# Evacuation of keys: both casts of ScalarE first, then both low parts of VectorE

## The chip, the cores and the metric

The kernel runs on one core of one Trainium2 chip. The metric is device time in microseconds (us) of one execution; times of the kernel before and after are medians of several runs. Engines are named as in the profile: PE is TensorE (matrix products), ACT is ScalarE, DVE is VectorE, POOL is GpSimd, SP is SyncE, which issues most DMAs.

## The reference, cut to what matters

One layer over 1024 tokens with width 1024. The input is normalised and modulated, then one projection gives queries, keys, values and gates for 16 heads of width 64: eight heads of forgetting attention (a softmax with a decay added to the scores) and eight of stick-breaking attention (a running product of sigmoids over the keys). The head outputs are gated, projected once more, added to the input and normalised again.

```python
h = u @ w_in[layer]
fq, fk, fv, fg, ff, sq, sk, sv, sg = _split_columns(h)
s = jnp.einsum('bhqd,bhkd->bhqk', q, k).astype(jnp.float32) * scale      # both kinds of heads
s = s + (f_q[..., :, None] - f_k[..., None, :])                          # forgetting heads
log_keep = jnp.where(strict, jax.nn.log_sigmoid(-z), 0.0)                # stick-breaking heads
y = jnp.concatenate([y_fox, y_sb], axis=-1) @ w_out[layer]
```

Everything is float32.

## The kernel before, in words

**Two parts for each number.** PE works here on a rounded 32-bit type (`F32R`). To keep more digits, the kernel splits an operand into a high part, which is the number rounded to that type, and a low part, the difference between the number and its high part. A product then takes several matmuls: high by high, low by high, high by low. The high part is usually a cast on ACT (or POOL), the low part a subtraction on DVE (or POOL).

**Pairs and chunks.** Heads are handled in eight pairs (`p`); a pair's two heads of 64 rows fill the 128 partitions. Pairs 0 to 3 are stick-breaking, 4 to 7 forgetting. For each pair the queries, keys and gates (`m` = 0, 1, 2) are projected in two chunks (`ch`) of 512 tokens. One chunk is 24 matmuls into one accumulator in PSUM (lines 255 to 257 in `m_step`); accumulators are a ring of two buffers (`acc_tile`). When the last matmul of a chunk is done, `evac_m` takes the result out of PSUM.

**Evacuation of keys.** `evac_k` handles a chunk of keys, once for each head in `heads`. Line 240 casts the head's 64 rows of the accumulator to the tile of high keys (`kst`, ACT). Line 242 copies these rows to the other 64 partitions of the same tile (a DMA on SP's queue). Line 243 subtracts the high part from the accumulator and writes the low keys (`klo`, DVE). It returns the last cast and the last subtraction, so that a caller can queue work behind them. Most calls handle both heads: one chunk of pair 0 in the first stage, the second chunks of pairs 0 and 1 after it, and both chunks of pairs 2 to 7 in the generator `gen_m`. Two calls, for the first chunk of pair 1, handle one head each, between other steps.

**Order of the work.** PE's instructions stay in the order in which the program writes them (`manual_schedule`); in the first stage SP's do too. For ACT, DVE, POOL and later SP, a planner chooses the order of instructions by a simulated clock, and adds the waits. In the main part, the attention of a pair runs unit by unit (a unit is one head and 128 queries), and the projections of later pairs fill PE's time in between (`fill`). For unit k the steps are: scores (`att_scores`, lines 410 and 411, one buffer for scores), their processing on ACT, DVE and POOL (lines 417 to 445), and two units later the transposes (line 461), split into a high part (line 463, ACT) and a low part (line 464, DVE), and the products with the values (line 476). In `att_pv` the products with the high part come first. Value projections (lines 310 to 312) use the same ring of accumulators.

Of the kernel before, what the change touches and what calls it, by code (L numbers as in the profile page):

```python
# [8 lines left out]
F32 = mybir.dt.float32  # L9
F32R = mybir.dt.float32r  # L10
AF = mybir.ActivationFunctionType
ALU = mybir.AluOpType
# [6 lines left out]
HD = 64  # L19
# [8 lines left out]
def tile_hybrid_layer(  # L28
# [17 lines left out]
    nc = tc.nc  # L46
# [188 lines left out]
    def evac_k(p, ch, acc, kst, klo, heads):  # L235
        s = slice(ch * 512, ch * 512 + 512)
        for h in heads:
            r = slice(h * HD, h * HD + HD)
            o = slice((1 - h) * HD, (1 - h) * HD + HD)
            first = nc.scalar.copy(kst[h][r, s], acc[r, :])  # L240
            kf = kst[h].bitcast(F32)
            nc.sync.dma_start(kf[o, s], kf[r, s])
            last = nc.vector.tensor_tensor(klo[r, s], acc[r, :], kf[r, s], op=ALU.subtract)  # L243
        return first, last

    def evac_g(p, ch, acc, sg):
# [12 lines left out]
    qst, kst, klo, sgt, vt = {}, {}, {}, {}, {}  # L259
# [11 lines left out]
    def evac_m(p, m, ch, acc, heads=(0, 1)):  # L271
        if m == 0:
            evac_q(p, ch, acc, qst[p], heads)
        elif m == 1:
            return evac_k(p, ch, acc, kst[p], klo[p], heads)
        else:
            evac_g(p, ch, acc, sgt[p])
# [364 lines left out]
    for kb in range(NB):  # L642
        last = kb == NB - 1
# [100 lines left out]
    for kb in range(NB):  # L744
# [13 lines left out]
        if kb < len(evacs):  # L758
            n, h = evacs[kb]
# [209 lines left out]
    for k in range(len(units) + LAG + 1):  # L969
        if k < len(units):  # L970
# [12 lines left out]
            p, h, i = units[k]  # L983
# [86 lines left out]
```

## Time and profile before

| what | us |
|---|---|
| median of 3 runs | 689.89 (689.56 to 691.04) |
| the profiled execution's own time | 689.48 |
| its span in the profile | 687.8 |
| PE busy | 673.6 (98% of the span) |
| DVE, ACT, POOL busy | 451.8, 381.9, 425.8 |
| all 32 casts of line 240 | median 0.58 each |
| all 32 subtractions of line 243 | median 0.69 each |

A row of the timeline gives the start in us from the start of the span, the duration, the engine, the line of the kernel, the operation, output and input, and in brackets the idle time of the engine before it with what released it. On ACT and DVE an instruction's duration overlaps the next one's by about 0.1 us. In the list of waits a row gives the engine and line that waited, what it waited for, the total in us, how often, and the longest. The granted clock of PE was 0.997 over the profiled execution.

### The profile page before, as it was taken

What the parts mean: (1) busy time and instruction counts of PE and PEld (TensorE: products, weight loads), DVE (VectorE), ACT (ScalarE), POOL (GpSimd) and SP (SyncE); (2) the same over time, 40 slices, a digit from 0 to 9 for tenths busy, and PEclk for the clock granted to TensorE, in tenths of its full rate; (3) what the DMA queues carried; (4) which work ended last, traced back from release to release, by engine and by line L of the source; (5) the groups of instructions that cost most, each with busy time, mean ns of one, the idle gap of its engine ahead of it and who ended that gap; (6) DMA issues with size and microseconds to landing.
All of it is one profiled execution on the core that took longest, in us unless ns stands there. A gap on an engine that the chain in (4) does not pass through costs nothing.

```text
span 687.8 us, 11790 instructions
## 1 busy us (share of the span) xinstructions
PE 673.6 (98%) x4033; PEld 589.1 (86%) x4033; DVE 451.8 (66%) x924; ACT 381.9 (56%) x862; POOL 425.8 (62%) x555
## 2 busy tenths in 40 slices
PE   7999999999999999999999999999999999999996
PEld 4789898888998888889998888889988889888885
DVE  6895458767656676767675665656565767774645
ACT  4666457856557666666674564655565666531000
POOL 4567978656438565557388887877584364665411
PEclk9999999999999999999999999999999999999998
DMA  8966231011102122112134553444341298143301
GB/s 306 416 235 246 67 110 57 25 41 53 39 9 70 41 55 55 38 47 62 30 133 150 177 170 109 152 152 147 101 135 54 66 296 350 56 157 117 129 31 61
DMA packets 44316, 81.60 MB, mean 119 GB/s; under 512 B 5152, under 2 KB 18784, under 8 KB 43616
## 3 DMA queue, kind: packets, MB, share of 16 engines
q1 hardware_dynamic: 43104, 76.65, 34.1%
q10 hardware_dynamic: 1152, 4.19, 2.1%
q8 instruction: 32, 0.52, 0.3%
q14 instruction: 28, 0.23, 0.1%
HBM read 60.34 MB, written 16.29 MB: 111 GB/s over the span
## 4 chain that ended last, share of the span: by engine, by line
PE 93%; DVE 2%; DMA 1%; POOL 1%; SPq 1%; ACT 1%; issue 0%; POOLq 0%; DVEq 0%
PE m L255 10%; PE pv L476 10%; PE m L256 10%; PE m L257 10%; PE T L461 9%; PE S L411 5%; PE S L410 5%; PE o L853 4%; PE o L851 4%; PE o L852 4%; PE v L310 4%; PE v L311 4%; PE v L312 4%; DMA wss<-in_w_ss_dram 1%; PE st_q L573 1%; PE st_late L569 1%
## 5 line engine op out<-in xcount | busy, mean ns | idle before, releaser
L255 PE MATMUL m<-uh,whi 128*128 128x512 f32 x304 | 126.5, 416 | 0.5 <-DVE kl L243 0.5
L257 PE MATMUL m<-uh,wlo 128*128 128x512 f32 x304 | 119.7, 394 | 0.0
L256 PE MATMUL m<-ul,whi 128*128 128x512 f32 x304 | 119.7, 394 | 0.0
L464 DVE TENSOR_TENSOR pt<-T,pt 128x512 fp32r<-128x512 f32 (+2 forms) x192 | 100.6, 551 | 17.9 <-ACT pt L463 16.8
L444 POOL TENSOR_TENSOR be<-be,kp 128x127 f32<-128x127 f32 (+3 forms) x64 | 77.1, 1206 | 33.7 <-DVE kp L440 24.0
L463 ACT CAST pt<-T 128x512 fp32r<-128x512 f32 (+2 forms) x192 | 85.7, 480 | 16.8 <-PE T L461 13.0
L436 DVE TENSOR_TENSOR_SCAN kp<-kp,floor 128x512 f32<-128x512 f32 (+2 forms) x64 | 65.2, 1018 | 32.1 <-ACT kp L430 31.2
L476 PEld LDWEIGHTS pv<-pt,v 128*128 128x128 f32 (+1 forms) x640 | 77.1, 163 | 4.5 <-DVE pt L464 0.7
L476 PE MATMUL pv<-pt,v 128*128 128x256 f32 (+3 forms) x640 | 80.4, 271 | 0.5 <-DVE pt L464 0.5
L425 POOL TENSOR_SCALAR a<-a,l 128x1024 f32<-128x1024 f32 (+3 forms) x64 | 48.0, 749 | 39.6 <-DVE l L424 26.0
L257 PEld LDWEIGHTS m<-uh,wlo 128*128 128x128 f32 x304 | 57.1, 188 | 13.6
L423 ACT ACTIVATE a<-a,nm 128x1024 f32<-128x1024 f32 (+3 forms) x64 | 49.8, 778 | 34.1 <-DVE nm L417 33.0
L410 PE MATMUL S<-k,q 128*128 128x512 f32 (+5 forms) x192 | 66.5, 348 | 0.2 <-DVE nm L417 0.2
L411 PE MATMUL S<-kl,qz 128*128 128x512 f32 (+5 forms) x192 | 65.5, 342 | 0.0
L255 PEld LDWEIGHTS m<-uh,whi 128*128 128x128 f32 x304 | 57.3, 188 | 9.2 <-DVE kl L243 0.9
L256 PEld LDWEIGHTS m<-ul,whi 128*128 128x128 f32 x304 | 57.4, 189 | 8.0
L497 POOL TENSOR_TENSOR ty<-ty,sg 64x256 f32<-64x256 f32 x64 | 47.4, 741 | 25.0 <-DVE ty L496 12.8
L417 DVE CUSTOM_DVE_ANT_0 a<-S,fb 128x1024 f32<-128x1024 f32 (+3 forms) x64 | 48.3, 755 | 20.5 <-PE S L411 9.8
L430 ACT ACTIVATE kp<-S 128x128 f32<-128x128 f32 (+3 forms) x64 | 41.7, 651 | 31.8 <-PE S L411 29.7
L310 PE MATMUL v<-whi_v,uh 128*128 128x256 f32 (+1 forms) x192 | 56.1, 292 | 0.7 <-DVE kl L243 0.7
L388 ACT CAST qz<-q 64x128 fp32r<-64x128 f32 x128 | 37.4, 295 | 32.9 <-PE S L411 31.8
L311 PE MATMUL v<-whi_v,ul 128*128 128x256 f32 (+1 forms) x192 | 54.2, 282 | 0.0
(291 smaller groups left out, 1609.6 us busy)
## 6 DMA issues: line engine op xcount, KB each, us to landing
raw<-in_w_qkg_dram SPq DMA_DIRECT2D x38, 256.0 KB, 3.0
wss<-in_w_ss_dram SPq DMA_DIRECT2D x5, 1024.0 KB, 9.0
x<-in_x_dram SPq DMA_DIRECT2D x8, 512.0 KB, 7.6
k<-k SPq DMA_DIRECT2D x32, 128.0 KB, 2.4
wg<-in_w_gate_dram SPq DMA_DIRECT2D x8, 512.0 KB, 4.5
raw_o<-in_w_out_dram SPq DMA_DIRECT2D x16, 256.0 KB, 2.7
fb<-f_dr ACTq DMA_DIRECT2D x8, 512.0 KB, 4.2
wo_dr<-whi_o SPq DMA_DIRECT2D x16, 256.0 KB, 2.7
```

Of the source, the lines that this page charges most:

```text
L255: nc.tensor.matmul(acc, hi[:, c], u_hi[kt][:, s], start=(kt == 0), stop=False)
L256: nc.tensor.matmul(acc, hi[:, c], u_lo[kt][:, s], start=False, stop=False)
L257: nc.tensor.matmul(acc, lo[:, c], u_hi[kt][:, s], start=False, stop=(kt == NB - 1))
L310: nc.tensor.matmul(acc[:, :n], u_hi[kt][:, ts_], hi[:, s], start=(kt == 0), stop=False)
L311: nc.tensor.matmul(acc[:, :n], u_lo[kt][:, ts_], hi[:, s], start=False, stop=False)
L410: nc.tensor.matmul(S[:, s, :w], qst[p][h][:, qs], kst[p][h][:, ks], start=True, stop=False)
L411: nc.tensor.matmul(S[:, s, :w], z, klo[p][:, ks], start=False, stop=True)
L436: scan = nc.vector.tensor_tensor_scan(rv, rv, floor[0][:, 512 - n:][:, ::-1], initial=0.0, op0=ALU.mult, op1=ALU.max)
L444: nc.gpsimd.tensor_tensor(be[:, :ke - 1], be[:, :ke - 1], kp[:, 1:ke], op=ALU.mult)
L463: nc.scalar.copy(hi[:, :n, qo:qo + P], t3)
L464: nc.vector.tensor_tensor(lo[:, :n, qo:qo + P], t3, hi.bitcast(F32)[:, :n, qo:qo + P], op=ALU.subtract)
L476: nc.tensor.matmul(acc[:m, q0:256], vt[p][:, kb, h * P:h * P + m], pt[:, kb % 4, q0:], start=start, stop=stop)
```

## The change

When a call of `evac_k` handles both heads, the program now writes both casts (each with its copy) first and both subtractions after them. Before, it wrote cast, copy, subtraction for head 0 and then the same for head 1. The instructions, their sizes and their tiles are the same. On ACT alone, on DVE alone and on SP's queue alone the instructions of one evacuation keep their sequence; what differs is how those of ACT and DVE stand to each other in the text.

```diff
             first = nc.scalar.copy(kst[h][r, s], acc[r, :])
             kf = kst[h].bitcast(F32)
             nc.sync.dma_start(kf[o, s], kf[r, s])
-            last = nc.vector.tensor_tensor(klo[r, s], acc[r, :], kf[r, s], op=ALU.subtract)
+        for h in heads:
+            r = slice(h * HD, h * HD + HD)
+            last = nc.vector.tensor_tensor(klo[r, s], acc[r, :], kst[h].bitcast(F32)[r, s], op=ALU.subtract)
         return first, last
```

## The prediction, made before the change was run

> **What bounds the kernel now.** I read the page first, then the list of what TensorE (PE) waited for, then who waits for whom around the two lines of the change, then the timelines of PE, ACT and DVE around each evacuation of keys.
>
> ```profile
> span 687.8 us, 11790 instructions
> PE 673.6 (98%) x4033; PEld 589.1 (86%) x4033; DVE 451.8 (66%) x924; ACT 381.9 (56%) x862; POOL 425.8 (62%) x555
> ...
> k<-k SPq DMA_DIRECT2D x32, 128.0 KB, 2.4
> ```
>
> The same order of matmuls with nothing late would take what it takes now less PE's waits. The list of those waits (total, times, longest) is short, and after the first 15 us of loading these are all the groups in it:
>
> ```profile
> PE T L461 <- DVE pt L464: 0.8, 1, 0.8
> PE v L310 <- DVE kl L243: 0.7, 1, 0.7
> PE pv L476 <- DVE pt L464: 0.5, 1, 0.5
> PE m L255 <- DVE kl L243: 0.5, 1, 0.5
> PE S L410 <- DVE nm L417: 0.2, 1, 0.2
> ```
>
> They sum to 2.7 us. Two of the five, 1.2 us, name line 243, the low part of the keys: PE waits there for an accumulator (two buffers) whose last reader is the second low part. So the change can gain about 1.2 us at those two places, 2.7 us if all five went, and no more without other matmuls; what it can lose has no such cap.
>
> How the evacuation runs today is seen where nothing else is on either engine (ACT and DVE timelines: start, duration, operation, idle before and its releaser):
>
> ```profile
> 77.35 0.58 ACT L240 CAST k<-st_late 64x512 fp32r<-64x512 f32 x1 [0.76 <-DVE q L232]
> 78.68 0.58 ACT L240 CAST k<-st_late 64x512 fp32r<-64x512 f32 x1 [0.75 <-DVE kl L243]
> ...
> 77.97 0.68 DVE L243 TENSOR_TENSOR kl<-st_late,k 64x512 fp32r<-64x512 f32 x1 [0.65 <-ACT k L240]
> 79.30 0.69 DVE L243 TENSOR_TENSOR kl<-st_late,k 64x512 fp32r<-64x512 f32 x1 [0.65 <-ACT k L240]
> ```
>
> Cast 0, low part 0, cast 1, low part 1 go strictly one after the other. Cast 1 needs nothing from low part 0, but both read the same accumulator, and cast 1 starts 0.03 us after low part 0 ends (77.97 + 0.68 = 78.65). A handover costs 0.03 to 0.04 us. From first start to last end: 79.99 - 77.35 = 2.64 us.
>
> **The change part by part.** It adds and removes no instruction. Of 17 calls that evacuate keys, 15 do both heads (the 32 copies of the page are 15 x 2 + 2); the two that do one head stay as they are. In the 15, cast 1 no longer stands behind low part 0, and low part 0 now stands behind cast 1, if the readers of one accumulator stay in the order of the text, as they are in the rows above. I take that.
>
> The spacings come from the evacuation at 457.61, whose rows serve again below:
>
> ```profile
> 457.61 0.58 ACT L240 CAST k<-m 64x512 fp32r<-64x512 f32 x1 [1.85 <-PE m L257]
> 458.09 0.47 ACT L463 CAST pt<-T 128x384 fp32r<-128x384 f32 x1
> ...
> 458.22 0.68 DVE L243 TENSOR_TENSOR kl<-m,k 64x512 fp32r<-64x512 f32 x1 [2.27 <-ACT k L240]
> 458.82 0.54 DVE L464 TENSOR_TENSOR pt<-T,pt 128x384 fp32r<-128x384 f32 x1
> 459.29 1.21 DVE L417 CUSTOM_DVE_ANT_0 a<-S,fb 128x1024 f32<-128x1024 f32 x1
> 460.53 0.69 DVE L243 TENSOR_TENSOR kl<-m,k 64x512 fp32r<-64x512 f32 x1
> ...
> 460.08 1.00 PE L476 MATMUL pv<-pt,v 128*128 128x256 f32 x8
> ```
>
> The instruction behind a cast starts 0.48 after it (458.09 - 457.61), the one behind a low part 0.60 after it (458.82 - 458.22). With t the start of cast 0: cast 1 runs from t + 0.48 to t + 1.06, low part 0 starts at t + 1.10 (it was t + 0.62), low part 1 at t + 1.70 and ends at t + 2.39. An undisturbed evacuation is 0.25 us shorter. The copy of head 1 across the partitions issues 0.85 us sooner (from t + 1.91 to t + 1.06), and DMAs behind it on SP's queue by up to that. It lands in 2.4 us. The nearest reader is the first scores, after the copy that issues at 78.68 + 0.58 today:
>
> ```profile
> 91.24 0.22 PE L410 MATMUL S<-k,q 128*128 128x128 f32 x1
> ```
>
> That is 12 us later, so I cost the copies and the queue at nothing; the cover is the projection work between, and would have to shrink to 3 us.
>
> *What goes.* The two accumulator waits:
>
> ```profile
> 171.05 0.58 ACT L240 CAST k<-m 64x512 fp32r<-64x512 f32 x1 [0.74 <-PE m L257]
> 174.11 0.58 ACT L240 CAST k<-m 64x512 fp32r<-64x512 f32 x1
> ...
> 175.67 0.69 DVE L243 TENSOR_TENSOR kl<-m,k 64x512 fp32r<-64x512 f32 x1
> 176.40 1.02 DVE L464 TENSOR_TENSOR pt<-T,pt 128x512 fp32r<-128x512 f32 x2
> ...
> 176.43 0.39 PE L310 MATMUL v<-whi_v,uh 128*128 128x264 f32 x1 [0.74 <-DVE kl L243]
> ...
> 550.14 0.58 ACT L240 CAST k<-m 64x512 fp32r<-64x512 f32 x1 [0.74 <-PE m L257]
> ...
> 552.72 0.69 DVE L243 TENSOR_TENSOR kl<-m,k 64x512 fp32r<-64x512 f32 x1
> 554.22 0.69 DVE L464 TENSOR_TENSOR pt<-T,pt 128x512 fp32r<-128x512 f32 x1
> ...
> 553.47 0.50 PE L255 MATMUL m<-uh,whi 128*128 128x512 f32 x1 [0.47 <-DVE kl L243]
> ```
>
> At 171.05 cast 1 came 3.06 us after cast 0 because other work of ACT had slipped in between; low part 1 ended at 176.36. After the change it ends at 171.05 + 2.39 = 173.44, and PE wants the buffer at 176.43 - 0.74 = 175.69: gone, 0.74 us. At 550.14 it ends at 552.53, PE wants 553.00: gone, 0.47 us. Together -1.21. What is late next at the first place are the differences of line 464; with a low part less ahead of them they end sooner than today's 177.42, so nothing of the 0.74 comes back.
>
> *What is held up.* ACT and DVE now do two things in a row where they had put something else between. ACT's next instruction comes up to 0.48 later, DVE's up to 0.48 + 0.60 later. I followed all 12 evacuations of the main part; at eight the delayed work has over 1 us to spare before PE, at four not.
>
> First, at 261.79, line 431 frees the only scores buffer, with little in hand:
>
> ```profile
> 262.76 0.59 ACT L431 ACTIVATE be<-S 128x512 f32<-128x512 f32 x1
> ...
> 263.68 0.31 PE L410 MATMUL S<-k,q 128*128 128x320 f32 x1
> ```
>
> It ends at 263.35; 0.48 later is 263.83, and with a handover PE starts at 263.87 instead of 263.68: +0.19.
>
> The other three are differences of line 464, the low part of the transposed weights, just ahead of the products (pv) that read them; pv does its high products first (5, 7 and 3 here) at 0.11 us each, then needs the low ones.
>
> ```profile
> 314.05 0.58 ACT L240 CAST k<-m 64x512 fp32r<-64x512 f32 x1 [0.67 <-PE m L257]
> ...
> 315.44 1.00 DVE L464 TENSOR_TENSOR pt<-T,pt 128x512 fp32r<-128x512 f32 x2
> ...
> 316.16 1.47 PE L476 MATMUL pv<-pt,v 128*128 128x256 f32 x12
> ...
> 405.11 0.56 ACT L240 CAST k<-m 64x512 fp32r<-64x512 f32 x1
> ...
> 405.50 0.40 PE L411 MATMUL S<-kl,qz 128*128 128x512 f32 x1
> ...
> 406.31 0.67 DVE L417 CUSTOM_DVE_ANT_0 a<-S,fb 128x512 f32<-128x512 f32 x1
> 406.92 1.14 DVE L464 TENSOR_TENSOR pt<-T,pt 128x512 fp32r<-128x512 f32 x2
> ...
> 407.13 1.97 PE L476 MATMUL pv<-pt,v 128*128 128x256 f32 x16
> ```
>
> At 314.05 the low parts start at 315.15 and 315.75, the first difference at 316.35, ending (0.69) at 317.04. PE needs it at 316.16 + 5 x 0.11 = 316.72, and gets it at 317.08: +0.36. At 405.11 line 417 can go at 405.94 (its scores are done at 405.90), then low parts at 406.55 and 407.15, first difference 407.75 to 408.44; PE needs it at 407.13 + 7 x 0.11 = 407.90: 408.48 makes +0.58. At 457.61 the low parts start at 458.71 and 459.31, and from 459.91 DVE has both line 464 and line 417 waiting. Difference first: it ends at 460.45, PE needs it at 460.08 + 3 x 0.11 = 460.41: +0.08. Line 417 first: 1.14 more (its start to the next start is 460.43 - 459.29 and the idle before it is none), +1.22. I take the first, since the difference is ahead of the scores in the text; both stay in the range.
>
> The Trainium skill (PSUM — Partial Sum Buffer, section Engine vs sequencer instructions) says that the queues of ScalarE and VectorE are strictly first in, first out: by it a low part that waits at the head holds all behind it, which speaks against the change. The trace agrees as far as it goes: ACT stands 0.75 us before the cast at 78.68.
>
> **Sum**: -0.74 - 0.47 + 0.19 + 0.36 + 0.58 + 0.08 = 0.00 us. The profiled execution took 689.48 us around its span of 687.8, the median of the runs is 689.89, 0.41 above it; the forecast is the median unchanged, **689.9 us**. Bounds: without any hold-up -1.21; with line 417 first +1.14.
>
> **The rivals.** (a) *Gain alone*: the planner, which orders ACT and DVE by its own clock, keeps the differences ahead of the low parts, as it does today at 458.82, and the accumulators still come free in time (2.2 and 0.47 us in hand): 689.89 - 1.21 = 688.7. Against: both low parts become ready before the differences at 314 and 457.
>
> (b) *A new wait in place of the old one, slower*: DVE takes the low parts and then also the next scores ahead of the differences: 0.58 + 0.23 at 405 (line 417 behind the low parts, 406.19 + 1.20 + 0.61 = 408.00 instead of 407.75), 1.22 at 457, 0.36 and 0.4 more at 314 (a short scan slips in), 0.19 at 261. That is 2.98 - 1.21 = +1.8: 691.7. It decides from 2.6 us of new PE waits (1.21 + 1.38). For it: cast 1 at 174.11, though first in the text, stands behind work that was ready sooner, so the planner serves by readiness. Against: four places must all fall that way.
>
> (c) *Everything re-planned*: shifted times change the order on ACT, DVE and POOL well beyond the 15 places, and the other three waits (1.5 us) go too: 689.89 - 2.7 = 687.2. Nothing in the trace ties those waits to keys; they end on lines 464 and 417.
>
> (d) *Low part 0 isn't tied to cast 1*: it starts at t + 0.62 as now, 0.48 sooner than assumed. The losses at 314, 405 and 457 shrink to about 0, 0.10 and 0, that at 261 stays: -0.92, 689.0. The Trainium skill (same page, section PSUM bank collisions raise a hardware error) says that readers of different 32-partition quadrants of a bank don't collide, and the heads are 64 partitions apart; the row at 78.68 shows them kept apart all the same, so the trace is stricter.
>
> (e) *It doesn't do what it says*: the planner leaves cast 1 behind other work: 689.9.
>
> **How the numbers follow.** Chances: forecast 0.40, (a) 0.20, (b) 0.20, (c) 0.11, (d) 0.05, (e) 0.04. A measurement of this kernel can tell about 0.2%, 1.4 us, from no change. Forecast, (d), (e) and most of (a) lie within; (c) and a fifth of (a) below; most of (b) above. Faster 0.15, same 0.66, slower 0.19. The range takes in (a) and (b) and leaves out (c) and the far tail of (b): 688.1 to 691.8.
>
> **What would show it.** Right: casts of one evacuation 0.48 apart and low parts 0.60 apart; PE's list without line 243; new short waits for line 464 near 316, 408 and 460 and for line 431 near 263. Wrong: cast 1 still behind lines 430 or 423; waits on line 243 that persist; waits above 0.3 us far from an evacuation (then (c), or its reverse). The prediction is wrong if the time leaves the range, or if it holds because nothing moved rather than because two movements cancel.

## The result, and the profile after

| | before | after |
|---|---|---|
| median, us | 689.61 (5 runs) | 692.18 (5 runs) |
| ratio, 95% interval | | 1.0038 (1.0026 to 1.0049) |
| span of the profiled execution, us | 687.8 | 690.7 |
| PE busy, us | 673.6 | 674.5 |

The change makes the kernel slower by 2.57 us, 0.38%. The forecast was no change, 689.9, and the time lies just outside the range of 688.1 to 691.8. (The forecast started from the first three of the five runs of before, whose median is 689.89.) Lines of the code from the old 244 on are two higher after the change: 245 is the low part of the keys, 397 the causal mask added for a later unit, 412 and 413 the scores, 419 their first step on DVE (the old 417), 433 the second sigmoid, 463 the transposes, 465 and 466 their high and low part, 478 the products with the values. The page counts 16 instructions more than before; all of them are semaphore instructions of the sequencers.

The page of the kernel after, and its list of PE's waits (total, times, longest):

```profile
span 690.7 us, 11806 instructions
PE 674.5 (98%) x4033; PEld 589.3 (85%) x4033; DVE 452.3 (65%) x924; ACT 383.4 (56%) x862; POOL 426.4 (62%) x555
...
PE pv L478 <- DVE pt L466: 3.5, 4, 1.5
...
PE T L463 <- DVE pt L466: 0.8, 1, 0.8
PE S L412 <- ACT be L433: 0.3, 1, 0.3
PE T L463 <- POOL be L447: 0.3, 1, 0.3
PE S L412 <- DVE nm L419: 0.2, 1, 0.2
```

Both waits for the low part of the keys are gone. In their place stand waits of the products for the low part of the transposed weights (0.5 us in one wait before, 3.5 us in four now) and one of the scores for the sigmoid. One of the four is the old wait near 115 us. The other three, and the wait of the scores, are at the four places which the prediction named. Apart from 0.3 us near 97 us, where the transposes wait for POOL right after the first stage (experiment 1 has the changed order there too, and not this wait), there is no new one in the main part. ACT, DVE and PE at these places (rows as before; "x2" is two instructions in a row):

```profile
261.19 1.19 ACT L240 CAST k<-m 64x512 fp32r<-64x512 f32 x2 [0.85 <-PE m L259]
262.40 0.60 ACT L432 ACTIVATE kp<-S 128x512 f32<-128x512 f32 x1
...
263.54 0.41 PE L412 MATMUL S<-k,q 128*128 128x320 f32 x1 [0.30 <-ACT be L433]
...
314.06 1.19 ACT L240 CAST k<-m 64x512 fp32r<-64x512 f32 x2 [0.67 <-PE m L259]
315.27 0.86 ACT L465 CAST pt<-T 128x512 fp32r<-128x512 f32 x2
...
315.28 1.39 DVE L245 TENSOR_TENSOR kl<-m,k 64x512 fp32r<-64x512 f32 x2 [0.33 <-ACT k L240]
316.70 1.02 DVE L466 TENSOR_TENSOR pt<-T,pt 128x512 fp32r<-128x512 f32 x2
...
317.45 0.98 PE L478 MATMUL pv<-pt,v 128*64 128x256 f32 x7 [0.59 <-DVE pt L466]
...
406.79 0.69 DVE L419 CUSTOM_DVE_ANT_0 a<-S,fb 128x512 f32<-128x512 f32 x1 [0.63 <-POOL ty L499]
407.41 1.39 DVE L245 TENSOR_TENSOR kl<-m,k 64x512 fp32r<-64x512 f32 x2
408.82 0.29 DVE L397 TENSOR_TENSOR fb<-fb,ps_causal 128x128 f32<-128x128 f32 x1
409.03 1.15 DVE L466 TENSOR_TENSOR pt<-T,pt 128x512 fp32r<-128x512 f32 x2
...
409.77 1.21 PE L478 MATMUL pv<-pt,v 128*64 128x256 f32 x9 [0.92 <-DVE pt L466]
...
459.50 1.19 ACT L240 CAST k<-m 64x512 fp32r<-64x512 f32 x2 [1.85 <-PE m L259]
460.71 0.48 ACT L465 CAST pt<-T 128x384 fp32r<-128x384 f32 x1
...
460.72 1.39 DVE L245 TENSOR_TENSOR kl<-m,k 64x512 fp32r<-64x512 f32 x2 [2.87 <-ACT k L240]
462.14 1.23 DVE L419 CUSTOM_DVE_ANT_0 a<-S,fb 128x1024 f32<-128x1024 f32 x1
463.29 0.55 DVE L466 TENSOR_TENSOR pt<-T,pt 128x384 fp32r<-128x384 f32 x1
...
460.33 0.40 PE L413 MATMUL S<-kl,qz 128*128 128x512 f32 x1
463.90 0.75 PE L478 MATMUL pv<-pt,v 128*64 128x256 f32 x5 [1.46 <-DVE pt L466]
```

At the first place the two casts run in a row, the sigmoids of lines 432 and 433 start behind them, and PE's scores wait for line 433. The other three show one picture: the two low parts run in a row, the difference of line 466 starts right behind them (or behind line 397 or 419 as well), and PE stops in the middle of a group of products until it is done.

How much each place cost is read from PE's own starts. PE's matmuls stand in the same order in both kernels, so the start of a scores matmul behind each place, after minus before, shows how far PE is late there. It is the first one behind the place, at pair 3 the second (line 413), since the first is the one that waits:

```
scores matmul after ...        before   after    late    step
the first stage                101.15   101.47   +0.32
pair 2, second chunk           181.51   180.91   -0.60   -0.92
pair 3, second chunk           263.82   263.79   -0.03   +0.57
pair 4, second chunk           319.65   320.45   +0.80   +0.83
pair 5, second chunk           410.98   412.87   +1.89   +1.09
pair 6, second chunk           462.55   466.12   +3.57   +1.68
pair 7, second chunk           555.98   558.90   +2.92   -0.65
```

Two gains, 1.57 us together, and four losses, 4.17 us: 2.60 us in the main part, beside 0.32 from ahead of it. Between these places and after them the lateness changes by less than 0.1 us: the first matmul of the last stage is 2.92 us late too (574.59 and 577.51).

### The profile page after: what moved, and what is told of

Read it like the earlier page. It is cut to its first block, busy times and chain, and to the rows that moved or that the text cites. A ratio compares the mean times of both kernels' runs of the same rounds, so it can differ in the third digit from the quotient of the medians.

```text
span 690.7 us, 11806 instructions
## 1 busy us (share of the span) xinstructions
PE 674.5 (98%) x4033; PEld 589.3 (85%) x4033; DVE 452.3 (65%) x924; ACT 383.4 (56%) x862; POOL 426.4 (62%) x555
## 4 chain that ended last, share of the span: by engine, by line
PE 52%; DVE 1%; issue 0%; ACT 0%; POOL 0%; POOLq 0%; DVEq 0%
PE pv L478 6%; PE T L463 5%; PE m L257 5%; PE m L259 5%; PE m L258 5%; PE o L855 4%; PE o L853 4%; PE o L854 4%; PE S L413 3%; PE S L412 3%; PE v L312 2%; PE v L313 2%; PE v L314 2%; DVE a L419 0%; DVE kl L245 0%
```

## The experiments

**Theory H**: the four hold-ups on ACT and DVE carry the loss, by the steps of the table, and the two accumulator waits the gain. **Rival R**: the loss comes from elsewhere, the first stage or the re-planned order on POOL and SP. The first five kernels take the changed order in some evacuations only. Their one edit to `evac_k`, with PLACES a set of (pair, chunk):

```diff
+        casts_first = (p, ch) in PLACES
         for h in heads:
...
-            last = nc.vector.tensor_tensor(klo[r, s], acc[r, :], kf[r, s], op=ALU.subtract)
+            if not casts_first:
+                last = low(h)
+        if casts_first:
+            for h in heads:
+                last = low(h)
```

`low(h)` is the subtraction. The diffs of this section are shortened. Line numbers behind this place differ from kernel to kernel and are named by what they do.

**1. All but four.** PLACES is everything except (3, 1), (4, 1), (5, 1), (6, 1).

> The changed order everywhere except in four evacuations of the main part (second chunk of pairs 3, 4, 5 and 6), which keep the order of before. Theory H (four hold-ups: PE loses 0.46 + 0.83 + 1.09 + 1.68 us at these four, by how far its matmuls are shifted from before, and gains 0.92 + 0.65 at two others): the four losses go, the two gains stay, and the first stage keeps its +0.3: 692.2 - 4.1 = 688.1 us, faster than before by 1.3. Rival R (the loss comes from re-planned work elsewhere, the first stage or the order on POOL and SP): the time stays near 692.

Measured: 687.96 us against 689.62 before, ratio 0.9976 (0.9967 to 0.9985). Faster, as H has it (which counted 0.46 for pair 3, up to the first scores matmul; to the second it is the 0.57 of the table). In its list of PE's waits only the old one of the products is left, 0.6 us.

**2. Only those four.** PLACES = (3, 1), (4, 1), (5, 1), (6, 1).

> The mirror image: the order of before everywhere except in the second chunk of pairs 3, 4, 5 and 6, which have both casts first. Theory H: the four losses and nothing else, 689.6 + 4.1 = 693.7 us, slower than the whole change. Rival R: near 689.6 to 690.5, since 11 of the 15 evacuations are as before.

Measured: 694.21 us against 689.62, ratio 1.0066 (1.0052 to 1.0080), 0.5 above H's figure and clear of R. Of the 0.5, 0.34 stands in its profile ahead of the first of the four places. Its list of PE's waits has the new ones beside the old (here 485 is the products, 473 the differences, 239 the low part of the keys, 440 the second sigmoid):

```profile
PE pv L485 <- DVE pt L473: 3.5, 4, 1.5
...
PE v L319 <- DVE kl L239: 0.7, 1, 0.7
...
PE m L264 <- DVE kl L239: 0.5, 1, 0.5
PE S L419 <- ACT be L440: 0.3, 1, 0.3
```

The four waits of the products, one of them the old one, sum to the same 3.5 us as in the whole change.

**3. Only two.** PLACES = (2, 1), (7, 1).

> The order of before except in two evacuations, the second chunk of pairs 2 and 7, where PE had waited for the accumulator. Theory H: both waits on line 243 go and nothing is lost, 689.6 - 1.6 = 688.0 us (the visible waits alone would give 688.4). Rival R: no gain, 689.6, because what is late next takes the place of the two waits.

Measured: 688.20 us against 689.62, ratio 0.9978 (0.9969 to 0.9987). The gain is 1.4 us (the interval is 0.9 to 2.1), between the visible waits (1.2) and H's figure (1.6); in its profile PE gains 0.91 and 0.64 at the two places, the table's gains to 0.01. What is late next did not take it back. Kernels 1 and 3 both beat both versions; between them the runs do not decide.

**4. Only the first stage.** PLACES = (0, 0), (0, 1), (1, 1).

> The changed order in the first stage alone (first and second chunk of pair 0, second chunk of pair 1), the main part as before. Theory H: PE's first scores start 0.1 to 0.3 us later, 689.8 us. Rival R, in the form that the first stage carries the loss: 691 to 692.

Measured: 689.95 us against 689.62, ratio 1.0006 (0.9997 to 1.0015): not told from no change, and far from the loss. PE's first scores start at 91.24 us before, 91.36 after and between 91.28 and 92.31 in the profiles of the experiments, whatever the order there. So the +0.32 at the head of the table (0.12 of it at the first scores, the rest from the wait for POOL near 97 us) is of the size by which profiles differ anyway.

**5. One alone.** PLACES = (6, 1).

> The order of before except in one evacuation, the second chunk of pair 6. It measures one hold-up by itself. Theory H: one new wait of PE of 1.4 to 1.5 us before the products of line 476, and the time rises by 1.7 (wait plus about 0.2 that the shift of later matmuls shows beyond each wait): 691.3 us. If a wait costs only its visible length: 691.1. Rival R: within 0.3 of before.

Measured: 691.47 us against 689.51, ratio 1.0023 (1.0015 to 1.0032). The medians lie 1.96 apart; the ratio is 1.6 us, with an interval from 1.0 to 2.2. The time alone can't tell 1.5 from 1.7, the trace can. PE at the products, in the kernel with this one place (here 485 is the products, 470 the transposes):

```profile
459.85 0.46 PE L485 MATMUL pv<-pt,v 128*128 128x256 f32 x3
461.77 0.74 PE L485 MATMUL pv<-pt,v 128*64 128x256 f32 x5 [1.46 <-DVE pt L473]
462.35 0.39 PE L470 MATMUL T<-ident,a 128*128 128x128 f32 x2
```

and in the kernel before, whose group of eight products stands in the prediction with its start at 460.08:

```profile
460.92 0.38 PE L461 MATMUL T<-ident,a 128*128 128x128 f32 x2
```

From the first product to the transposes it took 0.84 us before and takes 2.50 us with the wait: 1.66 more, of which the view calls 1.46 idle. The view counts idle time from the end of the last matmul, 459.85 + 0.46 = 460.31, but the next one would have started before that end, since matmuls overlap: in the kernel before, the fourth product starts 0.30 after the first, which is 460.15 here. That makes 0.16; the other 0.04 went while the products started again.

**6. The difference ahead of the scores.** The changed kernel, with one order added after the evacuation of (6, 1):

```diff
-            rows = nc.vector.tensor_tensor_reduce(out=v3(a), in0=S[:, :ns, :w], in1=v3(f),
+            with after(diff):        # the last difference of line 466, for the next unit only
+                rows = nc.vector.tensor_tensor_reduce(out=v3(a), in0=S[:, :ns, :w], in1=v3(f),
```

> The changed kernel in all places, with one edit: after the evacuation of the second chunk of pair 6, VectorE takes the difference of line 464 ahead of the scores of line 417 (it took them the other way round). That is the order which the prediction had assumed. Theory H: the wait of 1.46 us there shrinks to 0.1 to 0.4, so 692.2 - 1.2 = 691.0 us. Rival: the two low parts alone cause the wait, and the order of 464 and 417 changes little, 692.0.

Measured: 691.14 us, that is 1.04 below the changed kernel's 692.18, and 1.0023 (1.0014 to 1.0032) against before. This interval and the changed kernel's (1.0026 to 1.0049) overlap, so the trace decides. DVE and PE at the place (241 low part of the keys, 480 difference, 431 scores, 493 products):

```profile
461.28 1.39 DVE L241 TENSOR_TENSOR kl<-m,k 64x512 fp32r<-64x512 f32 x2 [2.88 <-ACT k L247]
462.70 0.56 DVE L480 TENSOR_TENSOR pt<-T,pt 128x384 fp32r<-128x384 f32 x1
463.18 1.22 DVE L431 CUSTOM_DVE_ANT_0 a<-S,fb 128x1024 f32<-128x1024 f32 x1
...
463.31 0.76 PE L493 MATMUL pv<-pt,v 128*64 128x256 f32 x5 [0.32 <-DVE pt L480]
```

The wait falls from 1.46 to 0.32. The 1.14 us between are line 419's turn ahead of line 466 (1.15, from 462.14 to 463.29 in the changed kernel).

**7. Low parts behind the differences.** The changed kernel, but the low parts of (4, 1), (5, 1) and (6, 1) are written after the next transposes and queued behind their difference; both casts stay first.

```diff
+            if (p, ch) in ((4, 1), (5, 1), (6, 1)):
+                waiting.extend((low, h) for h in heads)
+                return first, None
...
-            att_transpose(u)
+            diff = att_transpose(u)       # returns its last difference
+            with after(diff):
+                for low, h in waiting:
+                    low(h)
```

> The changed kernel, but in the second chunk of pairs 4, 5 and 6 the two low parts are queued on VectorE behind the differences of line 464 that were held up; both casts stay first. Theory H (the place of the low parts on VectorE is what costs, not the casts): three of the four waits go or fall under 0.4 us, 692.2 - 3.0 = 689.2 us, with the wait near 263 us (ScalarE, line 431) still there. Rival C (the casts in a row hold ScalarE's line 463 and so the differences anyway): at most half of it comes back, above 690.7.

Measured: 688.86 us against 689.51, ratio 0.9988 (0.9979 to 0.9997), 3.3 below the changed kernel. At the first of the three places (478 difference, 241 low part, 491 products):

```profile
315.35 1.02 DVE L478 TENSOR_TENSOR pt<-T,pt 128x512 fp32r<-128x512 f32 x2 [0.95 <-ACT pt L477]
316.29 1.38 DVE L241 TENSOR_TENSOR kl<-m,k 64x512 fp32r<-64x512 f32 x2
...
315.63 1.47 PE L491 MATMUL pv<-pt,v 128*128 128x256 f32 x12
```

and at the third (247 casts, 477 high part, 431 scores):

```profile
457.08 1.19 ACT L247 CAST k<-m 64x512 fp32r<-64x512 f32 x2 [1.85 <-PE m L271]
458.29 0.48 ACT L477 CAST pt<-T 128x384 fp32r<-128x384 f32 x1
...
458.35 1.22 DVE L431 CUSTOM_DVE_ANT_0 a<-S,fb 128x1024 f32<-128x1024 f32 x1 [2.92 <-PE S L425]
...
459.55 1.30 PE L491 MATMUL pv<-pt,v 128*128 128x256 f32 x8
```

At the first PE runs its twelve products without a wait. The casts are in a row as in the changed kernel, so it is the low parts' turn on DVE that costs nearly all of the loss, not the casts' turn on ACT; rival C falls. A little is left of it at the third place: the high part is done at 458.77, the scores' step went ahead at 458.35, and the eight products take 1.30 instead of 1.00. PE loses 0.25 us there, where it lost 1.68. The wait of the scores near 263 us, where ACT is late, stays at 0.30.

**8. Heads in the reverse order.** The changed kernel, with `for h in heads[::-1]` in both loops.

> The changed kernel with the heads taken in the reverse order, head 1 (partitions 64 to 127) first, in both loops. Nothing else differs. In the changed kernel's timeline the second cast starts 0.61 after the first and the next instruction 0.60 after the second, where the prediction had 0.48 each; the low parts are 0.70 apart where it had 0.60. Theory P (an instruction whose rows start at another partition than those of the one before it on its engine starts 0.11 to 0.13 later): casts 0.61, then 0.48 to the next; low parts 0.71, then 0.60 to the next. What stands behind the pair comes 0.13 (ScalarE) or 0.11 (VectorE) sooner, and the four hold-ups of PE shrink by that much each: 692.2 - 0.5 = 691.7 us, inside the uncertainty of the time, so the spacings decide. Theory Q (two readers of one accumulator in a row, or two writers of half tiles, are slow as such): spacings and time as in the changed kernel, in either order.

Measured: 692.13 us against 689.66, ratio 1.0039 (1.0026 to 1.0051): the time does not decide, as foreseen. The spacings do:

```profile
313.43 1.19 ACT L240 CAST k<-m 64x512 fp32r<-64x512 f32 x2 [0.67 <-PE m L259]
314.52 0.85 ACT L465 CAST pt<-T 128x512 fp32r<-128x512 f32 x2
...
314.65 1.39 DVE L245 TENSOR_TENSOR kl<-m,k 64x512 fp32r<-64x512 f32 x2 [0.33 <-ACT k L240]
315.97 1.00 DVE L466 TENSOR_TENSOR pt<-T,pt 128x512 fp32r<-128x512 f32 x2
...
406.08 0.69 DVE L419 CUSTOM_DVE_ANT_0 a<-S,fb 128x512 f32<-128x512 f32 x1 [0.64 <-PE S L413]
406.81 1.39 DVE L245 TENSOR_TENSOR kl<-m,k 64x512 fp32r<-64x512 f32 x2
...
554.10 5.98 DMA k<-k
...
560.22 0.47 PE S L412
```

From the first cast to the instruction behind the pair it is 1.09 us here and 1.21 in the changed kernel (314.06 to 315.27); from the first low part to the difference 1.32 here and 1.42 there (315.28 to 316.70). A single cast lasts 0.58, so in both kernels the second cast of a pair starts 1.19 - 0.58 = 0.61 after the first; what follows, which starts at partition 0, comes 0.48 after a second cast that starts at partition 0 and 0.60 after one that starts at partition 64. Theory P holds, Q falls. Three of the four hold-ups shrank (0.30 to 0.17, 0.59 to 0.46, 1.46 to 1.33), the one behind line 397 did not (0.92 and 0.93), and that fits the same rule. There the first low part stands behind line 419, which starts at partition 0: it starts 0.73 after it here (406.08 to 406.81, at partition 64) and 0.62 in the changed kernel (406.79 to 407.41, at partition 0). What is won behind the pair is lost ahead of it.

The last two rows are from the chain of waits of this execution: a copy of keys of the last pair took 5.98 us to land, and its scores waited 1.51 us. The execution took 693.41 us; of the five other runs four took 691.66 to 692.25 and one 693.84. Whether such copies make the slower of these runs can't be said, since only one of them has a trace.

## Why the prediction was wrong, point by point

**The mechanism was right.** No longer is cast 1 tied behind low part 0, low part 0 waits for cast 1, and both accumulator waits vanish. Low part 0 starts 0.03 us after the end of cast 1 at 78.66 in the undisturbed evacuation:

```profile
77.47 1.19 ACT L240 CAST k<-st_late 64x512 fp32r<-64x512 f32 x2 [0.76 <-DVE q L232]
...
78.69 1.41 DVE L245 TENSOR_TENSOR kl<-st_late,k 64x512 fp32r<-64x512 f32 x2 [1.25 <-ACT k L240]
```

So rival (d) is out. The evacuation takes 80.10 - 77.47 = 2.63 us, not 0.25 less than the 2.64 of before as forecast.

**The four places were right, and there was no fifth.** Rivals (a), (c) and (e) are out: the gains came with losses, the other waits of before stayed, and the casts are adjacent.

**The step that failed is the sum: its terms for the hold-ups were too small, so that two movements did not cancel.** Its four terms for the hold-ups come to 1.21 us and measured 4.17; the gains, 1.21 by the prediction, measured 1.57. So the main part lost 2.60 us where the sum has 0.00. The largest miss is the term for 457.61, +0.08 where 1.68 was measured. The lateness that the prediction worked out beside the step measured:

```
place     predicted   measured   what was left out
261.79      +0.19       +0.57    ACT's spacing 0.25, the scores' start again 0.10
314.05      +0.36       +0.83    spacing of casts and low parts 0.35
405.11      +0.58       +1.09    spacing of low parts 0.21, line 397 ahead 0.21, line 419 0.07 later
457.61      +0.08       +1.68    spacing as at 314.05, 0.35, and line 419 ahead 1.15
gains       -1.21       -1.57    idle shown is less than idle lost
```

The spacing term: the prediction took 0.48 and 0.60 from rows where the next instruction starts at the same partition. The two heads of an evacuation start at partitions 0 and 64, so cast 1 and the instruction behind it are each 0.12 to 0.13 later, and the low part 1 and its successor 0.10 to 0.12 later. That is why casts stand 0.61 apart and low parts 0.70, not the 0.48 and 0.60 that the prediction gave as signs. Experiment 8 shows that it is the start and not the pair. The prediction's own rows had it: behind the low part of head 1 at 175.67, line 464 starts at 176.40, 0.73 later. At 405.11 the low parts wait for line 419 and not for a cast, so only their own spacing counts there. What the last column leaves is 0.02 to 0.12 us a line, and was not followed further. (Two hundredths in the prediction's arithmetic are off, without effect: 316.16 + 5 x 0.11 is 316.71, and 408.00 less 407.75 is 0.25.)

**The choice at 457.61 was wrong.** The prediction saw both orders of line 464 and line 417, priced the second at +1.22, and took the first because it stands first in the text. The changed kernel has the second. In its rows the scores are done at 460.73 (460.33 + 0.40), the high part which the difference needs only at 461.19 (460.71 + 0.48), and line 419 went first: that fits a planner that puts first what is ready first, which is argued from the rows and not tested by a run. The row named under rival (b) for just this rule, cast 1 at 174.11 behind other work, spoke for it. Experiment 6 shows this choice alone to be worth about 1.1 us of PE's wait and about 1.0 us of the time.

**Rival (b) came nearest**, with 691.7 forecast and 692.18 measured. The new waits sum to 3.27 us (0.30, 0.59, 0.92 and 1.46), over the 2.6 that it asked for. It had two of its three enlargements wrong in kind (no short scan slipped in at 314; at 405 line 417 still goes first and line 397 took its turn), and missed the spacing; their sum was near by luck.

**The copies and the queue** cost nothing in the changed kernel, but the cover was misread: the prediction took the scores of the first stage, 12 us on, for the nearest reader. In the last pair the casts end at 554.92 (553.73 + 1.19) and the first scores that read this chunk start at 559.36, 4.4 us on, and in experiment 8 one slow copy came too late.

```profile
553.73 1.19 ACT L240 CAST k<-m 64x512 fp32r<-64x512 f32 x2 [0.74 <-PE m L259]
...
559.36 0.40 PE L412 MATMUL S<-k,q 128*128 128x512 f32 x1
```

## What to carry to other kernels

What you put first on an engine is paid by what stands behind it: here, two operations in a row ahead of a result that the bottleneck needed within 1 us cost 4.17 us at four places, more than the 1.57 us of the two waits that they removed. Change the order only at the places where the bottleneck waits for this result (experiment 3: 1.4 us faster), not in a helper that is also called where it waits for something else. When an estimate of zero is the difference of a gain and a loss of the same size, price the loss with the order in which the rows show work to become ready, not with the order of the text, and take the spacings from rows of the same start partition.

## What the runs showed of the hardware

**An instruction that starts at another partition than the one before it on its engine starts later.** On ACT 0.61 against 0.48 us behind a cast of 64 x 512, on DVE 0.69 to 0.73 against 0.60 behind a subtraction. The Trainium skill (VectorE: DVE Perf Modes, section Two Vector instructions with no wait between them) states for VectorE that an instruction whose inputs or output start in another quadrant (a group of 32 partitions) than those before it is held until the earlier ones have finished. The trace agrees: a low part lasts 0.68 or 0.69 and its follower at another start partition starts 0.69 to 0.73 after it, behind its end, with 0.60 where the starts agree. On ACT, of which that section does not speak, the runs show the same.

**A wait of PE costs more than the idle time that is shown.** The matmuls overlap, so 0.16 us passes in experiment 5 before idle time begins to count: 1.46 shown is 1.66 lost, and the waits that went, 0.74 and 0.47, gave back 0.92 and 0.65. A short wait may not show at all: at the third place of experiment 7 PE loses 0.25 us, and the view marks no idle time.
